# One written order over two adjoining seven-product SwiGLU stages, with low halves and sums placed ahead of the next residual update

## The chip, the core and the metric

The kernel runs on one core of a Trainium2 chip as one launch. The metric is the device time of that launch in microseconds (us); lower is better. Engines are called by the profile's short names: PE (matrix multiply), DVE (vector), ACT (activation), POOL, and SP, which here only issues transfers.

## What is computed

A two-layer trunk over x of 512 tokens by 1024 channels, all in float32. Each layer is half a SwiGLU block, a token mixer, and half a SwiGLU block; the mixer is an SSD scan in layer 0 and an S5 diagonal state-space model in layer 1. A last RMSNorm ends it.

```python
def swiglu(h, w_in, w_out):                 # w_in 1024 x 5632, w_out 2816 x 1024
    gate, up = jnp.split(h @ w_in, 2, axis=-1)
    return (jax.nn.silu(gate) * up) @ w_out

for i in range(2):
    x = x + 0.5 * swiglu(rmsnorm(x, ffn1_norm[i]), ffn1_w_in[i], ffn1_w_out[i])
    x = x + (ssd_mixer, s5_mixer)[i](rmsnorm(x, mix_norm[i]), ...)
    x = x + 0.5 * swiglu(rmsnorm(x, ffn2_norm[i]), ffn2_w_in[i], ffn2_w_out[i])
return rmsnorm(x, final_norm)
```

## The kernel before

The six stages run in the order `f1_0`, `ssd`, `f2_0`, `f1_1`, `s5`, `f2_1`. The residual x is held transposed in eight tiles `xT[d]`, d = 0 to 7, of 128 channels by 512 tokens.

**Products in three passes.** Every float32 operand is split into a high half and a low half, both of a faster matmul type. `split_w` makes `whi` (a copy on ACT, line 226) and `wlo` (a subtraction on DVE, line 228) of a loaded weight block `wst`; a product is then `whi`*high, `whi`*low and `wlo`*high (lines 235 to 237). There are four `wst` buffers and three each of `whi` and `wlo`.

**The seven-product stage.** `f2_0`, `f1_1` and `f2_1` call `ffn7`. It works through the 22 blocks of 128 hidden channels in five parts of 5, 4, 4, 4 and 5 blocks. The first part makes gate and up by plain products; the others make them from seven half-size products in place of eight (lines 384 to 386). At the end of each part the hidden blocks are multiplied by `w_out` and added to the residual, in eight steps d:

- `part(d)` is the product of step d on PE, in one of four PSUM banks (`pos[d]`): 15 matmuls in a part of five blocks, 12 in one of four. For d = 0 and 1 the last block of both products is done behind the rest, since the last hidden block is late.
- `split(j + 2)` splits the weight block for step d + 2. `fetch_to` asks for blocks further ahead; SP issues them as `wst` buffers come free.
- `after(d)` updates the residual, `xT[d] += 0.5 * pos[d]` (line 597; in `f1_1` it also regroups the tokens, line 594). In the last part it then calls `nxt.take(d, hold=True)`, which prepares the next stage's input.

**`take` and what it holds back.** Where the next stage is a SwiGLU block (kind `hilo`: after `f2_0`) `take` makes the high half `hH` (ACT, line 173) and the square `sq` (ACT, line 160) at once. It returns a function `rest`, which makes the low half `hL` (DVE, line 182) and adds `sq` to the running sum `acc` (DVE, lines 165 and 167). For d = 7 nothing is added: the sum over channels is taken from `acc` and the last `sq` by PE. After `f1_1` (next: `s5`) there is no `hH` and no `hL`, and `take` writes x to DRAM; after `f2_1` there is a scaled copy `xg` (ACT, line 1544) in their place, which PE turns and DVE copies to the output tile `fo` (line 1550). The list `held` keeps one `rest` back: `after(d)` for d > 0 ends with the `rest` of step d - 1, behind update d and behind `take(d)`, and the `rest` of step 7 follows the loop.

**What sets the order.** Inside `tc.manual_schedule(engines=...)` the instructions of the named engines are issued in the order in which they are written. Elsewhere a list scheduler orders each engine by its own estimate of times. `ffn7` writes the order of all five engines (`engines=ALL`) from its first product to its last update. Each call has such a block of its own; its first two lines, which fetch and split the first weights, stand ahead of that block, where only PE is in written order. `f2_0` already splits the first two weight blocks of `f1_1` (`after_w`) and hands them on (`have`). So between the end of `f2_0`'s block and `f1_1`'s the scheduler may exchange instructions of DVE, ACT and SP.

In the s5 stage's preparation inside `f1_1`, `fill` items are taken by `pop()` at the end of `after(d)`. Those at d = 3, 5 and 7, and one behind the loop, call `res_w`, which splits a weight block on ACT (line 1353) and DVE (line 1361).

Of the kernel before, what the change touches and what calls it, by code (L numbers as in the profile page):

```python
# [30 lines left out]
def trunk_kernel(ctx, tc, x, ffn1_norm, ffn1_w_in, ffn1_w_out, mix_norm, ffn2_norm, ffn2_w_in, ffn2_w_out,  # L31
# [272 lines left out]
    def ffn7(pr, w_in, w_out, nxt, parts, fill=(), late=None, ring=None, pad=40, turn=None, after_w=(), have=None):  # L304
# [228 lines left out]
        with tc.manual_schedule(engines=ALL):  # L533
            todo = []

            def pops(n):
                for _ in range(n):
                    todo and todo.pop(0)()

            for p, (a, b) in enumerate(parts):  # L540
                out = AH, AL = [], []
                prev = None
                for f in range(a, b):
                    if p:
                        iteration(f, prev, b, out)
                        prev = pairs[f]
                        continue
                    pg, pu = mm_ps(), mm_ps()
                    proj(pg, whole[2 * f], pr.H, pr.L)
                    split(2 * f + 2)  # L550
                    fetch_to(2 * f + 5)
                    gt, up = sv.tile([128, T], F32, name="gt"), sv.tile([128, T], F32, name="up")
                    if f == 0:
                        pr.sums()
                    else:
                        pops((0, 1, 2, 2, 2)[f])
                        V.tensor_tensor(gt, pg, pr.rbc, op=OP.mult)
                        S.activation(gt, gt, AF.Silu)
                    proj(pu, whole[2 * f + 1], pr.H, pr.L)
                    split(2 * f + 3)  # L560
                    fetch_to(2 * f + 6)
                    if f == 0:
                        pr.finish()
                        V.tensor_tensor(gt, pg, pr.rbc, op=OP.mult)
                        S.activation(gt, gt, AF.Silu)
                        for k in range(4):
                            todo += build(k)
                    else:
                        pops((0, 2, 2, 2, 0)[f])
                    V.tensor_tensor(up, pu, pr.rbc, op=OP.mult)  # L570
                    gated(up, 1.0, gt, out)
                    pop()
                n = b - a
                last = b == FT
                pos, held = [], []
                steps = {}
                if not last:
                    def step(name):
                        return lambda: getattr(pairs[b], name)()
                    if p == 0:  # L580
                        new_pair()
                        new_pair()
                    steps = {0: ["five"], 3: ["add7", "six"], 4: ["s6", "add3"], 7: ["s12"]}

                def part(d, k0, k1):
                    h, lo = whole[at[p, d]]
                    proj(pos[d], (h[:, k0:k1], lo[:, k0:k1]), AH[k0:k1], AL[k0:k1], first=k0 == 0, last=k1 == n)

                def after(d):
                    pops(1)  # L590
                    if last and turn:
                        new = s5.pop("spare", None) or turn()
                        pv, xv = [a_.rearrange("p (k q) -> p k q", q=8) for a_ in (pos[d], xT[d])]
                        V.scalar_tensor_tensor(new.rearrange("p (q k) -> p k q", q=8), pv, 0.5, xv, op0=OP.mult, op1=OP.add)
                        s5["spare"], xT[d] = xT[d], new
                    else:
                        V.scalar_tensor_tensor(xT[d], pos[d], 0.5, xT[d], op0=OP.mult, op1=OP.add)
                    if last:
                        held.append(nxt.take(d, hold=True))
                        if d:  # L600
                            held.pop(0)()
                    for nm in steps.get(d, ()):
                        getattr(pairs[b], nm)()
                    if last:
                        nxt.flush(3)
                    pop()

                for d in range(KD):
                    j = at[p, d]
                    pos.append(mm_ps())  # L610
                    if d == 0:
                        part(0, 0, 1)
                        if prev:
                            prev.acc_u4()
                            prev.c22()
                        split(j + 2)
                        if prev:
                            mul(prev.A, prev.W[3], 6)
                            prev.silu0()
                            prev.silu1()  # L620
                            mul(prev.E, prev.W[4], 0)
                            prev.c21()
                            gated(prev.up, -1.0, prev.gt, out)
                            if last:
                                es7.close()
                                fetch_to(j + 4)
                                if late:
                                    late()
                        part(0, 1, n - 1)
                        continue  # L630
                    if d == 1:
                        part(1, 0, n - 1)
                        for e in range(2):
                            part(e, n - 1, n)
                        split(j + 2)
                        fetch_to(j + 5)
                        for e in range(2):
                            after(e)
                        continue
                    part(d, 0, n)  # L640
                    if d < KD - 1 or last:
                        split(j + 2)
                    fetch_to(j + 5)
                    after(d)
                pops(len(todo))
                if last:
                    held.pop(0)()
            while fill:
                fill.pop(0)()
            nxt.flush()  # L650
            if nxt.kind != "hilo":
                nxt.sums()
                nxt.finish()
# [898 lines left out]
        return rows  # L1552


    op_es = ExitStack()

    def prep_for(st):
        if st is None:
# [107 lines left out]
    for i, s in enumerate(stages[:-1]):  # L1666
# [9 lines left out]
        else:  # L1676
            L = int(s[-1])
            wi, wo = (ffn1_w_in, ffn1_w_out) if s[:2] == "f1" else (ffn2_w_in, ffn2_w_out)
            if s in s5_pre[:1]:
                ffn(pr, wi[L], wo[L], nxt, fill=pre0, ready=ready, done=done, early=early, pad=160)  # L1680
                pre_es.close()
            elif s in s5_pre:
                with tc.manual_schedule(engines=MAN):
                    have = ffn7(pr, wi[L], wo[L], nxt, ((0, 5), (5, 9), (9, 13), (13, 17), (17, 22)),
                                after_w=[(ffn1_w_in[1][:, c:c + 128], KD) for c in (0, FF)])
            elif stages[i + 1] == "s5":
                def late5():
                    s5["op"] = op_es.enter_context(tc.tile_pool(name="s5op", bufs=2, side="right"))
                    s5["sel"] = s5["op"].tile([128, 136], F32, name="sel", bufs=1)
                    G.memset(s5["sel"], 0.0)  # L1690
                    G.memset(s5["sel"].rearrange("p (a b) -> p a b", b=8)[:, :, 7:8], 1.0)
                    out_ops(0, 0)

                fill = [lambda: None] * 63
                fill[52] = lambda: (scan_ops(0, 2), scan_ops(1, 1))
                fill[53] = lambda: scan_ops(1, 2)
                fill[54] = lambda: out_ops(1, 0)
                fill[55] = lambda: (res_load(0), out_ops(0, 1))
                fill[56] = lambda: (res_load(1), out_ops(1, 1))
                fill[57] = lambda: (u_load(0), res_w(0))  # L1700
                fill[58] = lambda: (u_load(1), res_load(2), scan_ops(2, 1))
                fill[59] = lambda: (res_load(3), res_w(1))
                fill[60] = lambda: u_load(2)
                fill[61] = lambda: (u_load(3), res_w(2))
                fill[62] = lambda: res_w(3)
                with tc.manual_schedule(engines=MAN):
                    ffn7(pr, wi[L], wo[L], nxt, ((0, 5), (5, 9), (9, 13), (13, 17), (17, 22)), fill=fill, late=late5, ring=s5["ring"], pad=40,
                         have=have, turn=lambda: s5["op"].tile([128, T], F32, name="xn", bufs=1))
            else:
                def late():  # L1710
                    fin["p"] = ctx.enter_context(tc.tile_pool(name="fin", bufs=2, side="right"))

                with tc.manual_schedule(engines=MAN):
                    ffn7(pr, wi[L], wo[L], nxt, ((0, 5), (5, 9), (9, 13), (13, 17), (17, 22)), late=late)
# [35 lines left out]
```

## Time and profile before

| what | value |
|---|---|
| device time, three runs | 2059.98, 2058.32, 2055.90 us; median 2058.32 us |
| profiled execution | 2060.75 us, of which the traced span is 2059.0 us |
| mean granted PE clock | 0.986 |
| busy: PE / DVE / ACT / POOL | 97% / 73% / 46% / 11% of the span |
| `f2_0` ends, `f1_1` begins (first product with `hH`) | 1184.18 us |
| `f1_1`'s last product, s5's channel sums | 1536.05 us, 1538.63 us |
| `f2_1`'s last product | 2043.98 us |

A timeline row has the start in the span, the duration, engine, line and operation, then output and inputs with their shapes; a number in square brackets is how long the engine sat idle before it, and which instruction ended that. A row of the windows view has the stretch, its length, then the busy time of each engine with its instruction count, the granted PE clock (1.00 is full speed), the share of the DMA engines and GB/s. Matmuls overlap, so their starts and not their durations give the pace.

### The profile page before, as it was taken

The page shows a single profiled execution, that of the slowest core. Times are in us where ns is not written, and L with a number is a line of the kernel's source. Part 1 is how long each engine was busy: PE and PEld are TensorE (multiplying, and loading weights), DVE is VectorE, ACT ScalarE, POOL GpSimd, SP SyncE. Part 2 cuts the span into 40 slices and gives each one's busy share as a digit, 9 for nine tenths or more (in the row PEclk, how much of TensorE's full clock was granted, in tenths as well). Part 3 has the DMA queues.
Part 4 walks back from the last instruction along what each step waited for, and adds up shares of the span by engine and source line. Part 5 has one row for each costly group of instructions (what it writes and reads, how often), then busy time and mean ns, then how long its engine had stood idle before and what let it go on. Part 6 is the DMA issues. An engine that isn't in the chain of part 4 may idle for free. (4 is left out here: it accounts for less than half of the span.)

```text
span 2059.0 us, 32113 instructions
## 1 busy us (share of the span) xinstructions
PE 1998.4 (97%) x12477; PEld 1735.8 (84%) x12477; DVE 1495.8 (73%) x2677; ACT 943.9 (46%) x1613; POOL 224.2 (11%) x338
## 2 busy tenths in 40 slices
PE   8999999999999998999999999999995999999997
PEld 7887778878878887889999978999985788999996
DVE  6899995687875787776677668666767556866675
ACT  5324333466672564444444534444443433444453
POOL 1002322011111010001011000001101100100010
PEclk9999999999999999999999999999997999999999
DMA  7446775343333332355566326455766432754561
GB/s 181 127 122 164 172 186 128 101 118 111 112 100 111 100 92 61 115 139 114 130 154 151 90 81 165 114 124 137 184 201 195 154 94 69 175 133 114 131 141 67
DMA packets 410057, 265.47 MB, mean 129 GB/s; under 512 B 40008, under 2 KB 383088, under 8 KB 409904
## 3 DMA queue, kind: packets, MB, share of 16 engines
q1 hardware_dynamic: 383024, 202.60, 35.1%
q0 software_dynamic: 26560, 59.75, 13.9%
q8 instruction: 98, 1.61, 0.3%
q10 hardware_dynamic: 320, 1.06, 0.1%
q14 instruction: 55, 0.45, 0.1%
HBM read 215.06 MB, written 21.04 MB: 115 GB/s over the span
## 5 line engine op out<-in xcount | busy, mean ns | idle before, releaser
L226 ACT CAST whi<-wst 128x1024 fp32r<-128x1024 f32 (+3 forms) x354 | 315.8, 893 | 390.2 <-PE mm L236 299.0
L228 DVE TENSOR_TENSOR wlo<-wst,whi 128x1024 fp32r<-128x1024 f32 (+3 forms) x354 | 364.0, 1028 | 119.4 <-ACT whi L226 117.7
L235 PE MATMUL mm<-hH,whi 128*128 128x512 f32 x984 | 391.8, 398 | 0.0
L236 PE MATMUL mm<-hL,whi 128*128 128x512 f32 x984 | 386.8, 393 | 1.8 <-DVE hL L182 1.7
L237 PE MATMUL mm<-hH,wlo 128*128 128x512 f32 x984 | 385.7, 392 | 0.0
L237 PE MATMUL mm<-ah,wlo 128*128 128x512 f32 x704 | 274.7, 390 | 0.0
L235 PE MATMUL mm<-ah,whi 128*128 128x512 f32 x704 | 274.5, 391 | 0.0
L236 PE MATMUL mm<-al,whi 128*128 128x512 f32 x704 | 274.4, 390 | 0.0
L236 PEld LDWEIGHTS mm<-hL,whi 128*128 128x128 f32 x984 | 186.2, 189 | 41.1 <-DVE hL L182 3.0
L235 PEld LDWEIGHTS mm<-hH,whi 128*128 128x128 f32 x984 | 186.3, 189 | 40.2 <-issue 1.6
L237 PEld LDWEIGHTS mm<-hH,wlo 128*128 128x128 f32 x984 | 186.1, 189 | 39.9 <-issue 0.4
L384 PE MATMUL mm<-th,hH 128*128 128x256 f32 x612 | 173.5, 284 | 0.0
L386 PE MATMUL mm<-th,hL 128*128 128x256 f32 x612 | 173.2, 283 | 0.0
L385 PE MATMUL mm<-tl,hH 128*128 128x256 f32 x612 | 173.1, 283 | 0.0
L237 PEld LDWEIGHTS mm<-ah,wlo 128*128 128x128 f32 x704 | 132.1, 188 | 28.1 <-issue 0.6
L236 PEld LDWEIGHTS mm<-al,whi 128*128 128x128 f32 x704 | 132.3, 188 | 26.5 <-issue 0.2
L235 PEld LDWEIGHTS mm<-ah,whi 128*128 128x128 f32 x704 | 132.3, 188 | 26.1
L299 POOL DMA_DIRECT2D wu<-wst x51 | 43.1, 846 | 833.9 <-DMA wst<-in_ffn_w_in_dram 265.6
L384 PEld LDWEIGHTS mm<-th,hH 128*128 128x128 f32 x612 | 117.4, 192 | 2.4 <-ACT up L458 2.4
L385 PEld LDWEIGHTS mm<-tl,hH 128*128 128x128 f32 x612 | 117.5, 192 | 0.0
L386 PEld LDWEIGHTS mm<-th,hL 128*128 128x128 f32 x612 | 117.4, 192 | 0.0
L386 PE MATMUL mm<-th,wlo 128*128 128x256 f32 x408 | 115.5, 283 | 0.0
(393 smaller groups left out, 3926.0 us busy)
## 6 DMA issues: line engine op xcount, KB each, us to landing
wst<-in_ffn_w_in_dram SPq DMA_DIRECT2D x125, 512.0 KB, 4.3
wu<-in_ffn_w_in_dram SPq DMA_DIRECT2D x51, 512.0 KB, 5.8
wst<-in_ssd_in_proj_dram SPq DMA_DIRECT2D x48, 512.0 KB, 4.0
wst<-in_ffn_w_out_dram SPq DMA_DIRECT2D x72, 256.0 KB, 2.9
wst<-in_ffn_w_out_dram SPq DMA_DIRECT2D x48, 320.0 KB, 3.2
wu<-wst POOLq DMA_DIRECT2D x51, 256.0 KB, 4.5
ws<-wst POOLq DMA_DIRECT2D x51, 256.0 KB, 4.6
dec<-d_cs POOLq DMA_DIRECT2D x16, 512.0 KB, 4.4
```

Source lines behind the costliest of these rows:

```text
L226: S.copy(hi, st)
L228: V.tensor_tensor(lo, st, hi.bitcast(F32), op=OP.subtract)
L235: PE.matmul(ps, hi[:, k], H[k], start=first and k == 0, stop=False)
L236: PE.matmul(ps, hi[:, k], L[k], start=False, stop=False)
L237: PE.matmul(ps, lo[:, k], H[k], start=False, stop=last and k == n - 1)
L299: G.dma_start(dst, src, accum_op=OP.add)
L384: PE.matmul(ps[:, c0], hi[:, k], mh, start=first and k == 0, stop=False, skip_group_check=True)
L385: PE.matmul(ps[:, c0], hi[:, k], ml, start=False, stop=False, skip_group_check=True)
L386: PE.matmul(ps[:, c0], lo[:, k], mh, start=False, stop=k == 3, skip_group_check=True)
```

## The change

Three edits in `ffn7` and around its two calls:

1. In the last part, the held `rest` of step d - 1 is issued in front of update d, no longer behind `take(d)`.
2. At d = 1, in every part, the split of the weight block for step 4 is issued between `after(0)` and `after(1)`. It used to be issued at d = 2, whose own split call now finds it done.
3. One block of written order for all five engines is opened ahead of `f2_0`'s call and closed behind `f1_1`'s.

```diff
                 def after(d):
                     pops(1)
+                    if last and d:
+                        held.pop(0)()
                     if last and turn:
                         new = s5.pop("spare", None) or turn()
 ...
                     if last:
                         held.append(nxt.take(d, hold=True))
-                        if d:
-                            held.pop(0)()
 ...
                         split(j + 2)
                         fetch_to(j + 5)
-                        for e in range(2):
-                            after(e)
+                        after(0)
+                        split(j + 3)
+                        after(1)
                         continue
 ...
-    op_es = ExitStack()
+    op_es, region = ExitStack(), ExitStack()
 ...
             elif s in s5_pre:
+                region.enter_context(tc.manual_schedule(engines=ALL))
                 with tc.manual_schedule(engines=MAN):
                     have = ffn7(...)              # f2_0
 ...
                     ffn7(...)                     # f1_1
+                region.close()
```

## The prediction

> **What bounds the kernel now.** I read the page first, then the stretches of the seven-product stages, then the timelines of DVE, ACT and PE where one stage meets the next.
>
> ```profile
> span 2059.0 us, 32113 instructions
> PE 1998.4 (97%) x12477; PEld 1735.8 (84%) x12477; DVE 1495.8 (73%) x2677; ACT 943.9 (46%) x1613; POOL 224.2 (11%) x338
> ```
>
> PE is the bound. Inside a stage it has no gap: the first row below, for nearly all of `f2_0`, has PE busy 320.00 of 320.00 us at full clock (columns: stretch, length, busy time and count of PE, weight loads, DVE, ACT, POOL, then the clock).
>
> ```profile
> 864.00:1184.00 320.00, 320.00 (x2085) 293.87 (x2084) 226.93 (x358) 149.07 (x277) 28.89 (x34) 1.00 0.52 127
> 781.00:788.00 7.00, 6.59 (x31) 5.57 (x32) 7.00 (x12) 4.02 (x8) 0.00 (x0) 1.00 0.16 46
> 794.20:800.00 5.80, 5.78 (x44) 4.81 (x45) 3.09 (x6) 0.00 (x0) 0.00 (x0) 0.71 0.21 64
> 1191.00:1198.20 7.20, 7.06 (x78) 5.34 (x79) 3.26 (x15) 1.04 (x1) 0.00 (x0) 0.53 0.52 149
> ```
>
> So only the borders can pay or cost. DVE at the first border (`f2_0` to `f1_1`), chosen rows:
>
> ```profile
> 1164.62 1.28 DVE L597 SCALAR_TENSOR_TENSOR xT<-mm,xT 128x512 f32<-128x512 f32 x2
> ...
> 1172.47 0.68 DVE L597 SCALAR_TENSOR_TENSOR xT<-mm,xT 128x512 f32<-128x512 f32 x1
> 1173.07 0.74 DVE L182 SCALAR_TENSOR_TENSOR hL<-xT,cols,hH 128x512 fp32r<-128x512 f32 x1
> 1173.73 0.69 DVE L167 TENSOR_TENSOR acc<-acc,sq 128x512 f32<-128x512 f32 x1
> 1175.08 0.83 DVE L228 TENSOR_TENSOR wlo<-wst,whi 128x640 fp32r<-128x640 f32 x1 [0.66 <-ACT whi L226]
> 1175.82 0.69 DVE L597 SCALAR_TENSOR_TENSOR xT<-mm,xT 128x512 f32<-128x512 f32 x1
> ...
> 1183.26 0.69 DVE L597 SCALAR_TENSOR_TENSOR xT<-mm,xT 128x512 f32<-128x512 f32 x1
> ...
> 1187.34 0.68 DVE L597 SCALAR_TENSOR_TENSOR xT<-mm,xT 128x512 f32<-128x512 f32 x1
> ...
> 1188.60 0.69 DVE L167 TENSOR_TENSOR acc<-acc,sq 128x512 f32<-128x512 f32 x1
> 1189.20 1.22 DVE L228 TENSOR_TENSOR wlo<-wst,whi 128x1024 fp32r<-128x1024 f32 x1
> 1190.34 0.75 DVE L182 SCALAR_TENSOR_TENSOR hL<-xT,cols,hH 128x512 fp32r<-128x512 f32 x1
> ```
>
> ACT in the same step, and PE where `f1_1` begins (first product, its sixteenth matmul, the wait):
>
> ```profile
> 1173.19 0.72 ACT L173 ACTIVATE hH<-xT,cols 128x512 fp32r<-128x512 f32 x1 [1.50 <-DVE xT L597]
> 1173.82 0.61 ACT L160 ACTIVATE sq<-xT 128x512 f32<-128x512 f32 x1
> 1174.34 0.71 ACT L226 CAST whi<-wst 128x640 fp32r<-128x640 f32 x1
> ```
>
> ```profile
> 1184.18 0.39 PE L235 MATMUL mm<-hH,whi 128*128 128x512 f32 x1
> 1187.58 0.39 PE L235 MATMUL mm<-hH,whi 128*128 128x512 f32 x1
> 1191.14 0.59 PE L236 MATMUL mm<-hL,whi 128*128 128x512 f32 x1 [1.43 <-DVE hL L182]
> ```
>
> Two things are to be seen. First, update, `hH`, `sq`, the next `whi`, its `wlo`, the next update is one closed chain through two queues: 1172.47, 1173.19, 1173.82, 1174.34, 1175.08, 1175.82, that is 0.72 + 0.63 + 0.52 + 0.74 + 0.74 = 3.35 us a step. PE takes 15 matmuls for a step, 1187.58 - 1184.18 = 3.40 us. The chain just keeps pace. `hL` and `acc` lie beside it now: they fill time in which DVE would wait for `whi` anyway. Second, at the end `hL` of step 7 (1190.34) stands behind a `wlo` of `f1_1` (1189.20, 1.14 us), which is written behind it; PE waits 1.43 us, and then runs at clock 0.53 for 7.2 us, a loss of 7.2 x 0.47 = 3.4 us.
>
> **The change, edit 1: `rest` ahead of the update.** DVE's order in a step of the last part becomes `wlo`, `hL`, `acc`, update. Nothing is added, but `hL` and `acc` of step d - 1 now stand behind a `wlo` that waits for ACT, and in front of the update that ACT waits for. They enter the chain: `hL` takes a slot of 0.66 us (1173.07 to 1173.73), `acc` one of 0.60 (1188.60 to 1189.20). The step becomes 3.35 + 1.26 = 4.61 us against PE's 3.40.
>
> In `f2_0` by steps: update 0 stays at 1164.62. Update 1 had followed at once (x2 in its row); with edit 2 a whole chain lies between, some 4.4 us (the first sum is only a copy, 0.35 as an estimate): 1169.0. Step 2 has no split: 0.72 + 0.63 + 0.61 for `sq`, then `acc` 0.60, about 2.7 with the hand-overs: 1171.7. Updates 3 to 5 at 4.61: 1185.5. In steps 6 and 7 the weight block is 1024 wide; the old step was 1187.34 - 1183.26 = 4.08, the new one 4.08 + 1.26 = 5.34: update 7 at 1196.2, against 1187.34. From there 0.72 to `hH` and about 0.76 to `hL`: 1197.7. PE used `hL` 0.80 after its start (1190.34, 1191.14), so 1198.5 against 1191.14: **+7.4 us**. PE is stopped earlier too, by `wlo` of steps 5 to 7, and in all these pauses nothing else is left for it; but its own work is far less than the chain's, so the chain sets the end. The clock falls after this border as it did before it, and that 3.4 us I take as unchanged.
>
> The second border (`f1_1` to `s5`) and the end:
>
> ```profile
> 1516.72 1.08 DVE L594 SCALAR_TENSOR_TENSOR xn<-mm,xT 128x512 f32<-128x512 f32 x1
> ...
> 1521.06 1.08 DVE L594 SCALAR_TENSOR_TENSOR xT<-mm,xT 128x512 f32<-128x512 f32 x1
> ...
> 1524.26 1.08 DVE L594 SCALAR_TENSOR_TENSOR xT<-mm,xT 128x512 f32<-128x512 f32 x1
> ...
> 1528.56 1.08 DVE L594 SCALAR_TENSOR_TENSOR xT<-mm,xT 128x512 f32<-128x512 f32 x1
> ...
> 1531.75 1.08 DVE L594 SCALAR_TENSOR_TENSOR xT<-mm,xT 128x512 f32<-128x512 f32 x1
> ...
> 1535.31 1.08 DVE L594 SCALAR_TENSOR_TENSOR xT<-mm,xT 128x512 f32<-128x512 f32 x1
> ...
> 1536.83 1.02 DVE L594 SCALAR_TENSOR_TENSOR xT<-mm,xT 128x512 f32<-128x512 f32 x1
> 1537.70 0.83 DVE L167 TENSOR_TENSOR acc<-acc,sq 128x512 f32<-128x512 f32 x1
> ```
>
> ```profile
> 1522.24 0.64 ACT L160 ACTIVATE sq<-xT 128x512 f32<-128x512 f32 x1 [1.95 <-DVE xT L594]
> ```
>
> ```profile
> 1538.63 2.81 PE L198 MATMUL aux<-acc,sel 128*128 128x64 f32 x16 [2.19 <-POOL v L1404]
> ```
>
> ```profile
> 1540.38 0.43 SPq L1325 DMA_DIRECT2D U<-d_u  x1
> ```
>
> ```profile
> 2022.77 1.28 DVE L597 SCALAR_TENSOR_TENSOR xT<-mm,xT 128x512 f32<-128x512 f32 x2
> ...
> 2034.08 0.68 DVE L597 SCALAR_TENSOR_TENSOR xT<-mm,xT 128x512 f32<-128x512 f32 x1
> ...
> 2037.50 0.68 DVE L597 SCALAR_TENSOR_TENSOR xT<-mm,xT 128x512 f32<-128x512 f32 x1
> ...
> 2044.41 0.69 DVE L597 SCALAR_TENSOR_TENSOR xT<-mm,xT 128x512 f32<-128x512 f32 x1 [1.99 <-PE mm L237]
> ```
>
> In `f1_1` only `acc` enters: the step 1524.26 - 1521.06 = 3.20 becomes 3.80, the one with a `res_w` in it (1528.56 - 1524.26 = 4.30) becomes 4.90. Update 1: 1516.72 + 3.55 = 1520.3 (the copy again). Step 2, without split: 1.18 to `sq` (1521.06 to 1522.24), 0.64, 0.60: 1522.7. Then 3.80, 4.90, 3.80: update 5 at 1535.2. The step to update 6 (old 1535.31 - 1531.75 = 3.56, `res_w` and no split) gives 4.16: 1539.4. `acc` of step 6 starts 1.18 + 0.64 later, 1541.2, against 1537.70: +3.5 for PE's channel sums, which start 0.93 behind it. The sums take longer from a longer pause: 0 to 0.8 us, I take 0.5, since the pause doubles. **+4.0 us.** Update 7 itself comes 5.0 later (1541.8), and SP issues the last load of U behind the x that it writes; that load moves from 1540.38 to about 1545.4, its users by 4.0, so I count nothing, at most 1.
>
> In `f2_1` the step of 3.42 (2037.50 - 2034.08) becomes 4.02: updates at 2022.8, 2026.5, 2028.5, then 2040.6 for update 5. Steps 6 and 7 have no split and take about 2.0 each: 2044.6. Update 7 waited for PE (2044.41) and nearly still does. One `acc` leaves the tail behind it. **0**, between -0.4 and +0.5.
>
> **Edit 2: the split at d = 1.** One `whi` and one `wlo` move ahead of update 1; its load was asked for just above, so no transfer moves. In the last parts its price is in update 1 above. In the four other parts update 1 comes about 0.74 us (one `wlo` slot) later and its bank is wanted first at step 5; three steps of 12 matmuls lie between, 3 x 2.7 us. PE has no gap there (first window row): **0**; without that cover it would be 0.74 a part.
>
> **Edit 3: one written order.** It puts `hL` of step 7 back ahead of the 1.14 us `wlo`; the chain above is already counted so, and the gain is inside the +7.4. At the region's other end:
>
> ```profile
> 839.20 1.22 DVE L228 TENSOR_TENSOR wlo<-wst,whi 128x1024 fp32r<-128x1024 f32 x1
> 840.33 0.75 DVE L182 SCALAR_TENSOR_TENSOR hL<-xT,cols,hH 128x512 fp32r<-128x512 f32 x1
> ```
>
> This `wlo` is already inside an all-engine block of `f2_0`, and yet it precedes the SSD stage's last `hL`: a block is not pinned behind what precedes it. **0** there; pinned, its first split would come some us later, 0 to 3. SP's loads and POOL's transfers are already asked for in this order.
>
> **Sum.** 7.4 + 4.0 + 0 = +11.4 us. On the profiled execution's 2060.75 that is 2072.2; this one lies 2.4 above the median of the three runs, 2058.32, so I forecast **2069.7, rounded 2070 us**. By its bounds (clock at the first border -3.4 or +6.6, see below; -1.0 to +1.0 at the second; 0.9 for the rest) the likeliest case alone runs from 2065 to 2077.
>
> **Clock.** The rows show a pause of 1.43 us followed by clock 0.53, one of 1.98 (ahead of 794.20) by 0.71, and one of 1.81 (ahead of 781.41) by 1.00. [...]
>
> **Rivals.** *The clock stays up.* The largest pause that I work out at the first border is about 2.2 us (for `hL` of step 6); the 1.81 row speaks for it, the 1.43 row against. It takes 3.4 off: 2066. Chance 0.10. *The clock falls already inside the tail.* PE's stops in steps 5 to 7, 0.8 to 1.2 us each, halve it; a step then takes 6.8 us, more than the chain, from 1174: the eighth product ends at 1194.4, the first of `f1_1` (24 matmuls at 0.45) at 1205.3 and not 1198.7. +6.6: 2076. Chance 0.12; 1.43 is the shortest pause seen to do it. *The region changes nothing*, since the block inside decides: the `wlo` still slips ahead of `hL`, +1.1: 2071, chance 0.05. *Written order is not what is issued*: then the chain keeps 3.35 and edits 1 and 2 do nothing, the region gives 1.1: 2057, within 0.2%. Against it: each row above stands in written order. Chance 0.12. *Faster:* if ACT's `whi` did not stand behind `sq`, `hL` and `acc` would run in DVE's pauses; the border's wait of 1.43 goes, and with it the 3.4 of low clock, and 0.9 at the second: 2052.5. It decides from a step of at most 3.40; I have 4.61, and ACT's rows in the order `hH`, `sq`, `whi` speak against it. Chance 0.06.
>
> **Numbers.** Likeliest 0.55; with the three rivals of the same sign, slower has 0.82; same 0.12; faster 0.06. 0.2% is 4.1 us, about what a measurement of this kernel can tell from no change. The range 2061 to 2077 leaves out the last two rivals.
>
> **What would show it.** Right: in `f2_0`'s last part DVE in the order `wlo`, `hL`, `acc`, update with updates about 4.6 us apart; PE waits for `wlo` and `hL` there; the first product with `hH` some 4 us later than 1184.18 and `hL` of step 7 some 7 us later than 1190.34; before s5's sums PE idles about 4 us, not 2.19. Wrong: updates still 3.4 apart, or the wait at `f1_1`'s first product gone.

## Result and the profile after

| | before | after |
|---|---|---|
| median of the runs compared | 2059.15 us (2055.90 to 2061.28) | 2072.49 us (2071.69 to 2073.13) |
| profiled execution, its span | 2060.75 us, 2059.0 us | 2072.29 us, 2070.4 us |
| mean granted PE clock | 0.986 | 0.984 |

The ratio after/before is 1.0071, with a 95% interval of 1.0057 to 1.0085. The changed kernel is slower by 13.3 us by the medians, 11.5 us by the two profiled executions. One run of all was slow, one of the ten of e5_plain below (2212.49 us at a mean granted clock of 0.843); its ratio leaves that run out.

Engine busy times on the page of the changed kernel:

```profile
PE 2002.6 (97%) x12477; PEld 1735.5 (84%) x12477; DVE 1495.8 (72%) x2677; ACT 944.5 (46%) x1613; POOL 224.2 (11%) x338
```

PE is at work 4.2 us longer than before (1998.4) in a span that is 11.4 us longer, so most of the difference is idle time of PE. DVE at the first border of the changed kernel (updates, one whole step, the last low half):

```profile
1163.70 0.68 DVE L599 SCALAR_TENSOR_TENSOR xT<-mm,xT 128x512 f32<-128x512 f32 x1
...
1170.80 0.68 DVE L599 SCALAR_TENSOR_TENSOR xT<-mm,xT 128x512 f32<-128x512 f32 x1
...
1175.42 0.69 DVE L599 SCALAR_TENSOR_TENSOR xT<-mm,xT 128x512 f32<-128x512 f32 x1
1178.03 0.82 DVE L228 TENSOR_TENSOR wlo<-wst,whi 128x640 fp32r<-128x640 f32 x1 [1.93 <-ACT whi L226]
1178.77 0.74 DVE L182 SCALAR_TENSOR_TENSOR hL<-xT,cols,hH 128x512 fp32r<-128x512 f32 x1
1179.43 0.69 DVE L167 TENSOR_TENSOR acc<-acc,sq 128x512 f32<-128x512 f32 x1
1180.04 0.68 DVE L599 SCALAR_TENSOR_TENSOR xT<-mm,xT 128x512 f32<-128x512 f32 x1
...
1189.99 0.68 DVE L599 SCALAR_TENSOR_TENSOR xT<-mm,xT 128x512 f32<-128x512 f32 x1
...
1195.34 0.68 DVE L599 SCALAR_TENSOR_TENSOR xT<-mm,xT 128x512 f32<-128x512 f32 x1
1196.81 0.75 DVE L182 SCALAR_TENSOR_TENSOR hL<-xT,cols,hH 128x512 fp32r<-128x512 f32 x1 [0.79 <-ACT hH L173]
```

The order is `wlo`, `hL`, `acc`, update, and `wlo` now waits 1.93 us for `whi`, where it waited 0.66. The updates are 4.62 us apart (1175.42, 1180.04), and 5.35 in a step with the wide weight block (1189.99, 1195.34). PE there, from the first product with `hH` to the sums:

```profile
1187.60 0.50 PE L235 MATMUL mm<-hH,whi 128*128 128x512 f32 x1 [0.81 <-ACT whi L226]
...
1188.86 0.50 PE L237 MATMUL mm<-hH,wlo 128*128 128x512 f32 x1 [0.53 <-DVE wlo L228]
...
1194.87 0.50 PE L236 MATMUL mm<-hL,whi 128*128 128x512 f32 x1 [1.88 <-DVE hL L182]
...
1196.83 0.79 PE L235 MATMUL mm<-hH,whi 128*128 128x512 f32 x1 [1.22 <-ACT hH L173]
1197.62 0.80 PE L236 MATMUL mm<-hL,whi 128*128 128x512 f32 x1
...
1198.77 0.61 PE L137 MATMUL aux<-ones,acc 128*32 128x1 f32 x32
```

PE pauses four times here, for `whi`, `wlo`, `hL` of step 6 and `hH` of step 7, and three times shortly before, for `whi` (0.21, 0.51 and 0.52 us ahead of 1173.43, 1178.05 and 1182.67). The kernel before had one wait of 1.43 us. The clock behind this border, in the changed kernel:

```profile
1196.00:1203.00 7.00, 6.17 (x75) 4.33 (x76) 5.05 (x17) 3.22 (x4) 0.00 (x0) 0.51 0.47 137
```

The loss of clock is 7.00 x 0.49 = 3.4 us, as before. DVE and POOL at the second border of the changed kernel:

```profile
1528.41 1.08 DVE L596 SCALAR_TENSOR_TENSOR xT<-mm,xT 128x512 f32<-128x512 f32 x1
...
1532.21 1.08 DVE L596 SCALAR_TENSOR_TENSOR xT<-mm,xT 128x512 f32<-128x512 f32 x1
...
1540.90 1.08 DVE L596 SCALAR_TENSOR_TENSOR xT<-mm,xT 128x512 f32<-128x512 f32 x1
1543.25 1.70 DVE L1362 TENSOR_TENSOR hL<-wst,hH 128x512 fp32r<-128x512 f32 x2 [1.27 <-ACT hH L1354]
1544.87 1.08 DVE L167 TENSOR_TENSOR acc<-acc,sq 128x512 f32<-128x512 f32 x1
1545.88 1.01 DVE L596 SCALAR_TENSOR_TENSOR xT<-mm,xT 128x512 f32<-128x512 f32 x1
```

```profile
1543.80 0.60 POOL L1393 COPY rh<-rho 128x504 f32<-128x504 f32 x1
...
1544.42 0.98 POOL L1393 COPY rh<-rho 128x504 f32<-128x504 f32 x1
```

A step is 3.80 us (1528.41 to 1532.21), the one to update 6 is 4.98 (1540.90 to 1545.88). PE at the second border and later in the changed kernel (channel sums, first users of U, start of `f2_1`, last transposes), then the same points of the kernel before that the prediction did not show:

```profile
1548.44 3.65 PE L198 MATMUL aux<-acc,sel 128*128 128x64 f32 x16 [4.75 <-issue]
...
1559.44 3.68 PE L1386 MATMUL aux<-U,opH 128*64 128x64 f32 x64 [3.94 <-DVE U L1380]
...
1711.58 0.50 PE L236 MATMUL mm<-hL,whi 128*128 128x512 f32 x1 [0.29 <-DVE hL L182]
...
2058.09 0.66 PE L1550 MATMUL aux<-ident,xg 128*128 128x128 f32 x4 [1.00 <-ACT xg L1545]
```

```profile
1548.80 3.69 PE L1385 MATMUL aux<-U,opH 128*64 128x64 f32 x64 [3.94 <-DVE U L1379]
...
1700.18 0.50 PE L236 MATMUL mm<-hL,whi 128*128 128x512 f32 x1 [0.28 <-DVE hL L182]
...
2046.49 0.66 PE L1549 MATMUL aux<-ident,xg 128*128 128x128 f32 x4 [0.81 <-ACT xg L1544]
```

The difference after minus before, read along the run:

| point | before | after | difference | added since the last |
|---|---|---|---|---|
| update 0 of `f2_0`'s last part | 1164.62 | 1163.70 | -0.92 | |
| norm row copied by ACT (`rbc`, line 212) | 1201.65 | 1207.42 | +5.77 | +6.69 |
| s5's channel sums | 1538.63 | 1548.44 | +9.81 | +4.04 |
| first users of U | 1548.80 | 1559.44 | +10.64 | +0.83 |
| `f2_1` begins | 1700.18 | 1711.58 | +11.40 | +0.76 |
| last transposes | 2046.49 | 2058.09 | +11.60 | +0.20 |

The instructions ahead of `f2_0` stand in the same order in both kernels, so the -0.92 is no effect of the change: in the nine traces that have `wlo` ahead of it, update 0 lies anywhere between 1163.15 and 1165.05.

### The profile page after: what moved, and what is told of

The parts are those of the page before. It is cut to its first block, busy times and chain, and to the rows that moved or that the text cites. A ratio compares the mean times of both kernels' runs of the same rounds, so it can differ in the third digit from the quotient of the medians.

```text
span 2070.4 us, 32125 instructions
## 1 busy us (share of the span) xinstructions
PE 2002.6 (97%) x12477; PEld 1735.5 (84%) x12477; DVE 1495.8 (72%) x2677; ACT 944.5 (46%) x1613; POOL 224.2 (11%) x338
## 4 chain that ended last, share of the span: by engine, by line
PE 55%; DVE 3%; ACT 2%; issue 1%; DMA 1%; POOL 0%; SPq 0%; ACTq 0%; POOLq 0%; DVEq 0%
PE mm L235 9%; PE mm L236 9%; PE mm L237 9%; PE mm L384 6%; PE mm L386 6%; PE mm L385 6%; PE aux L386 2%; PE aux L385 2%; PE aux L384 2%; PE aux L1419 1%; DMA U<-d_u 1%; ACT whi L226 1%; DVE xT L599 0%; PE aux L1386 0%; DMA wst<-in_s_glu_w_dram 0%
## 5 line engine op out<-in xcount | busy, mean ns | idle before, releaser
L415 DVE TENSOR_TENSOR hL<-ws,hH 128x512 fp32r<-128x512 f32 x102 | 69.6, 689 | 65.1 <-ACT hH L413 65.1
```

The source lines that it names most:

```text
L415: V.tensor_tensor(lo, src, hi.bitcast(F32), op=OP.subtract)
```

## The experiments

The theory: update, `hH`, `sq`, `whi`, `wlo` and the next update are a closed chain through ACT's and DVE's queues, and whatever DVE does in it one behind another is paid once a step. The main rival: the work put ahead of the update has slack, and the cost is somewhere else (the moved split, the written order over both stages, one border alone). Each kernel was timed beside the kernel before in its own group of runs, and the ratio is to that. The kernel before had medians of 2060.61 us beside e1 to e4, 2058.76 beside e5 to e8 and 2058.46 beside e9 and e10, so medians of different groups compare less well than ratios.

| run | what it is | median, us | ratio to before | 95% interval |
|---|---|---|---|---|
| e1_rest | edit 1 alone | 2072.66 | 1.0063 | 1.0051 to 1.0076 |
| e2_region | edit 3 alone | 2057.52 | 0.9987 | 0.9978 to 0.9996 |
| e3_split | edit 2 alone | 2060.21 | 0.9999 | 0.9991 to 1.0008 |
| e7_acc | edit 3, and `acc` ahead in `f2_0` | 2063.36 | 1.0021 | 1.0012 to 1.0029 |
| e8_both | edit 3, and `hL` and `acc` ahead in `f2_0` | 2069.76 | 1.0055 | 1.0042 to 1.0068 |
| e9_second | edit 3, and `acc` ahead in `f1_1` | 2062.56 | 1.0021 | 1.0012 to 1.0030 |
| e4_low | the change, `wlo` behind the update | 2055.39 | 0.9979 | 0.9969 to 0.9989 |
| e5_plain | edit 3, `wlo` behind the update | 2054.65 | 0.9979 | 0.9969 to 0.9990 |
| e6_best | e4_low, s5's sums ahead of the last fill item | 2052.60 | 0.9967 | 0.9956 to 0.9979 |
| e10_copies | the change, two POOL copies given to ACT | 2069.98 (one run) | | |

### The three edits one by one

**e1_rest: edit 1 alone.**

```diff
                     pops(1)
+                    if last and d:
+                        held.pop(0)()
...
                         held.append(nxt.take(d, hold=True))
-                        if d:
-                            held.pop(0)()
```

> Edit 1 alone: the held rest stands ahead of the update, no early split, no common region. Chain theory (hL and acc enter the closed chain update, hH, sq, whi, wlo, update): updates of f2_0's last part 4.6 us apart against 3.35, hL of step 7 about 1.1 us later still than in the changed kernel, because the next stage's wlo may again slip ahead of it; +12 to +14.5 us on the kernel before, so 2071 to 2074. Theory that the early split is the cost (update 1 starts 4.4 us late and never catches up): 0, within 2 us of before. Theory that the common region is the cost: 0.

Measured: 1.0063, which is the whole cost within the intervals. PE at the first border of this kernel:

```profile
1198.90 0.80 PE L236 MATMUL mm<-hL,whi 128*128 128x512 f32 x1 [0.54 <-DVE hL L182]
```

Without the region the `wlo` of `f1_1` slips ahead of the last `hL` again, and PE waits 0.54 us for it (this row), which the changed kernel does not. Counted from update 0, this `hL` is only 0.25 us later than in the changed kernel (33.36 us, 33.11), not 1.1 as expected, since DVE waits 0.79 us for `hH` there in the changed kernel.

**e2_region: edit 3 alone.**

```diff
             elif s in s5_pre:
+                region.enter_context(tc.manual_schedule(engines=ALL))
...
+                region.close()
```

> Edit 3 alone: one written order over f2_0 and f1_1, nothing else. Chain theory: updates stay 3.35 us apart; hL of step 7 moves ahead of the 1.14 us wlo, the wait of 1.43 us at the first border falls to about 0.3, and where the clock then stays up the 3.4 us behind it go too: -1.1 to -4.6 us. Theory that the common region is the cost: slower by most of the 13 us. Early-split theory: 0.

Measured: 0.9987, a gain of some 2.7 us. PE's only wait at the first border of this kernel, and DVE's updates and last `hL`:

```profile
1189.57 0.50 PE L236 MATMUL mm<-hL,whi 128*128 128x512 f32 x1 [0.30 <-DVE hL L182]
```

```profile
1175.39 0.68 DVE L597 SCALAR_TENSOR_TENSOR xT<-mm,xT 128x512 f32<-128x512 f32 x1
...
1178.75 0.68 DVE L597 SCALAR_TENSOR_TENSOR xT<-mm,xT 128x512 f32<-128x512 f32 x1
...
1188.77 0.74 DVE L182 SCALAR_TENSOR_TENSOR hL<-xT,cols,hH 128x512 fp32r<-128x512 f32 x1
1189.84 1.23 DVE L228 TENSOR_TENSOR wlo<-wst,whi 128x1024 fp32r<-128x1024 f32 x1 [0.32 <-ACT whi L226]
```

`hL` of step 7 (1188.77) is back ahead of the `wlo` (1189.84), the wait is 0.30 in place of 1.43, and the clock stays at 1.00. The step of the chain is the old one, 3.36 us.

**e3_split: edit 2 alone.**

```diff
-                        for e in range(2):
-                            after(e)
+                        after(0)
+                        split(j + 3)
+                        after(1)
```

> Edit 2 alone: the split for step 4 between the first two updates, in every part. Chain theory: update 1 of the last parts comes some 3.4 us later, but step 2 then has no split and takes only the time that is left, so updates 2 to 7 are about 0.5 us later than before: 0 to +1 us. Early-split theory: most of the 13 us. Region theory: 0.

Measured: 0.9999, no change within the interval (1.9 us down, 1.6 us up). Edit 2 alone costs nothing and brings nothing that these runs can tell.

### Which part of edit 1, and which border

**e7_acc and e8_both: the sum alone, then the low half and the sum, in `f2_0` only, over edit 3.** (`low` and `add` are the two halves of `rest`.)

```diff
+                    if last and d and after_w:
+                        held[0].add()              # e7_acc
+                        held.pop(0)()              # e8_both
...
-                        if d:
+                        if d and after_w:
+                            held.pop(0).low()      # e7_acc; nothing in e8_both
+                        elif d:
                             held.pop(0)()
```

> The written order over the region as in the run that has it alone, and on top of it, in the first stage's last part only, the sum (acc) of the slice before put right ahead of each update; the low half (hL) stays behind it. Theory (a closed chain over ACT and DVE; a step costs what DVE starts in it, one behind another): the step is 3.35 + the sum's 0.60 = 3.95 us in the update rows, 0.55 over PE's 3.40, so that over the part's steps the last update is some 4 us later (7 x 0.60 = 4.2) and the time 2057.5 + 4.2 = 2061.7, up to 2065.5 if the longer wait at the first border lowers the clock again. Rival (the low half is what hurts, since PE's third product reads it; the sum has slack): the update rows stay 3.35 to 3.40 apart and the time is that of the region alone, 2057.5.

> The same, with the low half and the sum ahead of each update in the first stage's last part only; the second stage keeps the old order. Theory: steps of 3.35 + 0.66 + 0.60 = 4.61 us, the first border some 7 us later than with the region alone, 2057.5 + 7 = 2064.5, up to 2068 with a lower clock at the border; what is left to the 2072.7 of edit 1 alone (5 to 8 us) is the second border and its sums. Rival (the whole cost is the first stage's chain): 2071 to 2073 already here. Rival (most of it is the second border): 2059 to 2061.

Two neighbouring updates on DVE in e7_acc, with the sum ahead of the second, then two in e8_both:

```profile
1178.69 0.68 DVE L607 SCALAR_TENSOR_TENSOR xT<-mm,xT 128x512 f32<-128x512 f32 x1
...
1182.05 0.68 DVE L167 TENSOR_TENSOR acc<-acc,sq 128x512 f32<-128x512 f32 x1
1182.65 0.68 DVE L607 SCALAR_TENSOR_TENSOR xT<-mm,xT 128x512 f32<-128x512 f32 x1
```

```profile
1179.61 0.69 DVE L607 SCALAR_TENSOR_TENSOR xT<-mm,xT 128x512 f32<-128x512 f32 x1
...
1184.22 0.68 DVE L607 SCALAR_TENSOR_TENSOR xT<-mm,xT 128x512 f32<-128x512 f32 x1
```

From update to update:

| step of the chain | 640-wide block | 1024-wide block |
|---|---|---|
| old order (e2_region) | 3.36 | 4.08 |
| `acc` in it (e7_acc) | 3.96 | 4.68 |
| `hL` and `acc` in it (e8_both) | 4.61 | 5.34 |

The chain adds 0.60 and 0.66 us a step, the time that DVE needs from one instruction to the next. That settles the mechanism, and the rival with slack for the sum falls: `acc`, which PE reads only when the stage's steps are done, costs by itself 0.0034 of the time (7 us by the ratios, 5.8 by the medians; 7.5 at `rbc` by the two traces, counted from update 0), of it 3.4 us of low clock that came with the longer wait (the expectation allowed 4.2 to 8 together).

e8_both came out at 2069.8 where at most 2068 was expected. Against e2_region its `rbc` (1207.38) and its sums in s5 (1544.36) are both 10.3 us later, which is what the expectation allowed (7 us and the lower clock). Another 1.9 us comes between the sums and the start of `f2_1`: 0.9 of it while the sums run, at a clock of 0.53 in 3.45 us where e2_region took 2.56 us behind the same pause of 2.19 us, and 1.1 behind the first users of U. That last stretch, up to the start of `f2_1`, takes 150.6 to 153.7 us in the twelve traces with no relation to the edits (151.38 before, 152.14 changed, 153.45 in e1_rest, 151.36 in e10_copies), so a difference of 1 us in it says nothing about them.

**e9_second: `acc` ahead in `f1_1` only, over edit 3.**

```diff
+                    if last and turn and d:
+                        held.pop(0)()
...
-                        if d:
+                        if d and not (last and turn):
                             held.pop(0)()
```

> The written order over the region, and the sum put ahead of the next update in the second stage's last part only; the first stage keeps the old order, and no split is moved between the first two updates (so the second update still follows the first at once). Theory (a closed chain here too, of 3.80 and 4.90 us a step in place of 3.20 and 4.30, with about 0.8 more in the step that ends beside POOL's two copies): the channel sums start 3 to 4 us later behind the last product than with the region alone, PE's pause ahead of them grows from 2.19 to about 4.5 us, and the time is 2057.5 + 3 to 5 = 2060.5 to 2062.5. Rival (the second border is hidden, the whole cost lies at the first): the same 2057.5 within 1 us.

PE's pause ahead of the channel sums in this kernel:

```profile
1538.98 3.64 PE L198 MATMUL aux<-acc,sel 128*128 128x64 f32 x16 [4.75 <-issue]
```

The pause is 4.75 us as in the changed kernel, though the first border is untouched here (`rbc` 0.86 us later than in e2_region, update 0 too). Beyond that 0.86 the sums are 4.06 us later than in e2_region (1534.06 there) and the users of U 5.14 (1549.98 against 1543.98): the second border costs 5.1 us by itself. The medians give 5.0, the ratios 0.0034 or 7 us; 3 to 5 was expected. Counted from update 0, the users of U come 5.1 us later than in e2_region here, 12.1 in e8_both and 16.0 in the changed kernel (1559.44), so the two borders (17.2 us together) account for the whole cost.

### Cutting the chain

**e4_low: the whole change, but in the last parts `wlo` is issued behind the update.** `split` becomes two halves; the second is called from `after(d)`.

```diff
...                                                # the steps 0 and 1 likewise
-                    if d < KD - 1 or last:
+                    if last:
+                        split_hi(j + 2)            # whi on ACT
+                    elif d < KD - 1:
                         split(j + 2)
                     fetch_to(j + 5)
-                    after(d)
+                    after(d, j + 2)                # ends its update with split_lo(j + 2): wlo on DVE
```

> The changed kernel with one thing more in the last part of each seven-product stage: whi of the split stays where it is, but its wlo is issued behind the update, so DVE's order is hL, acc, update, wlo. The same instructions, and rest still ahead of the update. Chain theory: wlo no longer waits behind sq with the update behind it, the chain is cut (update, hH, sq, acc, update: 0.72 + 0.63 + 0.64 + 0.60 = 2.6 us, DVE alone 2.6, both under PE's 3.40), so PE sets the pace: updates 3.4 apart, no wait at the first border, clock 1.00 there, sums at the second border 1 to 3 us earlier than before. All 13 us go and 4 to 8 more: 2051 to 2056. Theory that rest ahead of the update costs in itself, or that the early split or the region does: about as slow as the changed kernel, 2070 to 2073.

**e5_plain: the same cut, with edit 3 but without edits 1 and 2.**

> The written order over the region, low halves and sums behind the update as in the kernel before, no weight split moved between the first two updates; only the low half of the weight (wlo) is put behind the update in both last parts, as in the run that did this on top of the whole change. Theory (wlo is what closes the chain from update to update; with it behind the update PE is the bound, whatever else stands ahead): update rows 3.40 apart waiting for PE, the first border without a wait, time 2054 to 2057, the same as that run's 2055.4 within 1.5 us. Rival (low half and sum ahead of the update are worth something once the chain is cut, at the second border's sums): 2 to 4 us longer than that run, 2057 to 2059.

Updates on DVE in e4_low and one low half, then an update in e5_plain:

```profile
1168.82 0.75 DVE L182 SCALAR_TENSOR_TENSOR hL<-xT,cols,hH 128x512 fp32r<-128x512 f32 x1 [0.79 <-ACT hH L173]
...
1176.39 0.69 DVE L617 SCALAR_TENSOR_TENSOR xT<-mm,xT 128x512 f32<-128x512 f32 x1 [0.56 <-PE mm L237]
...
1179.79 0.69 DVE L617 SCALAR_TENSOR_TENSOR xT<-mm,xT 128x512 f32<-128x512 f32 x1 [0.56 <-PE mm L237]
```

```profile
1177.55 0.69 DVE L615 SCALAR_TENSOR_TENSOR xT<-mm,xT 128x512 f32<-128x512 f32 x1 [0.71 <-PE mm L237]
```

In both these updates are 3.40 us apart (the one ahead of 1177.55 was at 1174.15) and wait for PE, in whichever order the rest stands; both come to 0.9979, and PE has no wait at the first border in either. A loop through both engines is still there in e4_low, since `hL` waits for ACT's `hH` (0.79 us at 1168.82). But with `whi` and `wlo` out of it the loop is short: where the updates do not wait for PE (1167.35, 1170.09 and 1172.99) they are 2.74 us apart in a step without a split and 2.90 in one with it, less than PE's 3.40. So the same `hL` and `acc` ahead of the update that cost 13 us cost nothing that these runs can tell. e4_low came out near the slow end of the 2051 to 2056 expected, and its second border shows a new wait, in PE and in DVE:

```profile
1541.78 3.36 PE L1407 MATMUL aux<-U,opH 128*64 128x64 f32 x64 [7.69 <-DVE U L1401]
```

```profile
1536.68 1.29 DVE L1383 TENSOR_TENSOR hL<-wst,hH 128x512 fp32r<-128x512 f32 x2 [2.83 <-ACT hH L1375]
1537.89 0.22 DVE L121 TENSOR_SCALAR nw_v<-aux 128x64 f32<-128x64 f32 x1
```

PE idles 7.69 us ahead of the first product with U: the sums are issued right behind the last product (1530.34) and take less than 4 us, but the steps behind them (1537.89) stand on DVE behind a low half that waited for a transfer through ACT.

**e6_best: e4_low with those steps issued ahead of that last fill item.**

```diff
-            while fill:
-                fill.pop(0)()
             nxt.flush()
             if nxt.kind != "hilo":
                 nxt.sums()
                 nxt.finish()
+            while fill:
+                fill.pop(0)()
```

> The whole change with wlo behind the update, and the second stage's sums with the steps behind them issued ahead of the last weight split that fills the stage's end (the one whose low half waits for a transfer). Theory: in the run without this the steps behind the sums began at 1537.89, behind that low half, 3.7 us after the sums were done; here they begin right behind the sums, and the first product of the next stage (1541.78 there) can start up to 3.7 us sooner: 2051.7 to 2054.5, less where the next stage's own weight lands only then. Rival (that weight lands at about 1541.4 in any case and is the bound): the same 2055.4, within 0.7 us, with the wait now put down to a DMA.

DVE and PE of e6_best at the same place:

```profile
1535.06 0.23 DVE L121 TENSOR_SCALAR nw_v<-aux 128x64 f32<-128x64 f32 x1 [0.25 <-PE aux L198]
...
1538.10 1.29 DVE L1383 TENSOR_TENSOR hL<-wst,hH 128x512 fp32r<-128x512 f32 x2
```

```profile
1540.04 3.40 PE L1407 MATMUL aux<-U,opH 128*64 128x64 f32 x64 [5.02 <-DVE U L1401]
```

The pause is 5.02 us, 2.67 less, and the time 2052.6 us, ratio 0.9967: the lowest here, though its interval still touches that of e4_low. The rest of the expected 3.7 us stayed because the low half (1538.10, 1.2 us) still stands ahead of DVE's scaling of U (1539.30).

### The step that was too long

**e10_copies: the whole change, POOL's two copies made by ACT.** In the changed kernel the step 1540.90 to 1545.88 took 4.98 us where 4.16 was forecast; its `hL` pair took 1.70 us and its `acc` 1.08, beside POOL's copies at 1543.80 and 1544.42 (shown above).

```diff
-                G.tensor_copy(rh[:, :, 1:], ...)
+                (S.copy if i < 2 else G.tensor_copy)(rh[:, :, 1:], ...)
```

> The whole change, with the two copies of 128x504 (line 1393, output rh) that POOL makes at the second border made by ACT instead, for the first two groups of s5. Theory (the last low half of two, 1.70 us, and the sum behind it, 1.08 us, are long because POOL's copies run beside them): they take 1.29 and 0.68 us, as those rows do elsewhere, the step to the update after them takes 4.16 in place of 4.98 us, and the channel sums start 0.8 us sooner behind the first border; the time gains at most that, less than can be measured. Rival (these rows are long for another reason, the transfers beside them): 1.70 and 1.08 us stay.

DVE in e10_copies:

```profile
1540.68 1.08 DVE L596 SCALAR_TENSOR_TENSOR xT<-mm,xT 128x512 f32<-128x512 f32 x1
1543.03 1.29 DVE L1362 TENSOR_TENSOR hL<-wst,hH 128x512 fp32r<-128x512 f32 x2 [1.27 <-ACT hH L1354]
1544.24 0.68 DVE L167 TENSOR_TENSOR acc<-acc,sq 128x512 f32<-128x512 f32 x1
1544.84 1.02 DVE L596 SCALAR_TENSOR_TENSOR xT<-mm,xT 128x512 f32<-128x512 f32 x1
```

1.29 and 0.68 us, and the step is 4.16: the 0.82 us came from POOL's copies. PE's sums start at 1547.40, 0.83 us sooner behind the first border than in the changed kernel (`rbc` at 1207.21). In the changed kernel the pair of low halves (1.70 for 1.29) and the sum (1.08 for 0.68) took 0.4 us more each beside the copies, and POOL's second copy took 0.98 us where the first took 0.60.

## Why the prediction was right, point by point

The forecast of 2070.0 us is 2.5 us below the median of 2072.49, inside the range and nearest to the likeliest case; the sum of +11.4 us compares with +11.5 between the profiled executions and +13.3 between the medians (11.7 to 17.5 by the interval of the ratio). That 11.4 and 11.5 agree so closely is partly luck: the changed kernel's profiled execution was 0.92 us ahead at update 0, and from there the table above adds up to 12.5, with one term 0.7 too large and others too small by 0.9, 0.8 and 0.2.

- **The chain and its step:** forecast 4.61 and 5.34 us, measured 4.62 and 5.35. With the 0.92 us added by which the run was ahead, update 1 (1168.05) stands at 1168.97, forecast 1169.0; update 2 (1170.80) at 1171.72, forecast 1171.7; update 7 (1195.34) at 1196.26, forecast 1196.2; the last `hL` (1196.81) at 1197.73, forecast 1197.7.
- **First border, +7.4:** PE's use of that `hL` came at 1197.62, +6.48 and with the 0.92 +7.40, as forecast. But the step "that 3.4 us I take as unchanged" was off by 0.7: 6.69 were left at `rbc`. The low clock lasts as long as before (0.50 for 6.8 us in both, by stretches of 1 us), but began near 1196, ahead of step 7's product, so that PE stood still in part of it; behind the start of the sums (1198.77) 4 us of it were left, where before there were 6 behind 1192.09. PE's stops in the tail were put down to `wlo`; the rows put 0.21, 0.51, 0.52 and 0.81 us to `whi` and 0.53 to `wlo`, which changes nothing in the sum, since the chain sets the end.
- **Second border, +4.0:** measured +4.9, that is 4.04 at the sums (forecast 3.5) and 0.83 from the sums to the users of U (0.5). The mis-sized term is the step to update 6, forecast as 3.56 + 0.60 = 4.16 and measured as 4.98; e10_copies shows what it left out, POOL's copies, which the later chain brought beside two groups of DVE instructions. Updates 1, 2 and 5, less 5.77, came at 1520.25, 1522.64 and 1535.13 (forecast 1520.3, 1522.7, 1535.2). That U's users move with the sums, and not with the load of U, held. The reason given for the 0.5, that a longer pause makes the sums slower, was an estimate that names no row, and the runs bear it out only in part: behind 4.75 us the sums took 3.65 and 3.64 us (the changed kernel, e9_second), but behind the same pause of 2.19 us 2.56, 2.81 and 3.45 in e2_region, the kernel before and e8_both, and behind 2.83 us 1.97 in e3_split.
- **`f2_1`'s end, 0:** +0.2; its updates 2034.18, 2037.87 and 2039.86, less 11.40, came at 2022.78, 2026.47 and 2028.46 (forecast 2022.8, 2026.5, 2028.5). **s5 between the borders:** not in the sum, measured +0.76, within the scatter of that stretch over the twelve traces (150.6 to 153.7 us).
- **Edit 2, 0:** e3_split shows it, 0.9999. **Edit 3:** alone it gives 2.7 us (e2_region), where the wait is 0.30 us and the clock stayed at 1.00; in the changed kernel the chain's waits take that away. What is left of it, against e1_rest and counted from update 0, is 0.25 us at the last `hL` and 0.92 at `rbc` (44.64 us against 43.72), too little to tell the two kernels apart by time. The forecast had put that rest at 1.1.
- **The rivals:** the clock did not stay up (0.51 in the row at 1196) and did not fall in the tail (1.00 up to 1196, through pauses of 0.81, 0.53 and 1.88). The region did act (the 0.54 of e1_rest is gone). Written order was issued (`wlo`, `hL`, `acc`, update in the rows above). The faster rival's condition, a step of at most 3.40, was met in e4_low and e5_plain, where `whi` and `wlo` are out of the loop: 2055.4 and 2054.7, against its 2052.5.

The 2.5 us between forecast and median: the runs of the kernel before reach from 2055.9 to 2061.3 us, and the profiled one, from which the terms were taken, lies 1.6 above their median. The one trace of that kernel shows the clock fall at its first border (3.4 us); whether it fell there in the other runs is not shown.

## What to carry to other kernels

Before moving work of an in-order engine ahead of an instruction, look for a loop of waits through that instruction: add up one turn of it, and compare with the pace of the engine that bounds. Here, where the loop was the slower of the two, work that stood in it was paid in full at each turn, though DVE was busy only 73% of the time; work beside it was free. Moving the work back is one remedy (0.9987 with edit 3, in e2_region); another was to shorten the loop by taking a wait for the other engine (`wlo` behind `whi`) out of it, until PE's pace was the slower (0.9979 in e4_low, 2.90 us a step against 3.40). Then the next wait in line, DVE's steps behind a late low half, was worth moving too.

## What the runs showed of the hardware

**The low clock cost the same each time at the first border.** Behind the first border the kernel before lost 7.20 x 0.47 = 3.4 us of clock after a pause of 1.43 us, the changed kernel 7.00 x 0.49 = 3.4 after pauses of 1.88 and 1.22, and e7_acc, after one of 2.40, 9.00 x 0.38 = 3.4:

```profile
1194.00:1203.00 9.00, 9.00 (x87) 6.78 (x86) 4.54 (x16) 1.92 (x2) 0.00 (x0) 0.62 0.48 138
```

The clock fell at this border in six traces (the kernel before, the changed kernel, e1_rest, e7_acc, e8_both, e10_copies), and in each the stretch from 1188 to 1206 has a mean clock of 0.81, a loss of 18.00 x 0.19 = 3.4 us. In e3_split a wait of 1.44 us at the same place left the clock at 1.00, so that it isn't the length alone that decides; what does, no run here shows. By stretches of 1 us the clock stood at 0.50 for 6.8 us in each of the five traces read so (the kernel before, the changed kernel, e1_rest, e7_acc, e8_both), which is the same 6.8 x 0.50 = 3.4 us.

**What POOL's copies cost differed with what DVE did beside them.** In the kernel before, the same two copies stood at 1536.55 and 1537.39, beside an update, which takes one of its inputs from PSUM (1536.83, 1.02 us, no longer than its 1.08 elsewhere), and one sum (1537.70, 0.83 us for 0.68). The changed order put them beside instructions with both inputs in SBUF (the pair of low halves at 1543.25 and the sum at 1544.87), and the same copies cost 0.82 us. That the place of the inputs is the cause, no run here shows.

**A float32 product of the same form held PE three times as long as one of the split halves.** In the kernel before, at a clock of 1.00, the three float32 matmuls of line 832 (`aux<-wx,btok`, 128x256, two records each, from 447.51) held PE for 1.11 us up to the next product (448.62), 0.37 us each; matmuls of the split halves in that form (lines 384 to 386) start 0.12 us apart (1902.64, 1902.76).
